# Seven block products in layer 0 as well, with two weight sums made by accumulating transfers

## The chip, the cores and the metric

The kernel runs on one core of a Trainium2 chip. The metric is the time of one execution on the device in microseconds (us), the median of several runs. The engines are TensorE (PE; its weight loads are shown apart as PEld), VectorE (DVE), ScalarE (ACT), GpSimd (POOL) and SyncE (SP), which issues the plain transfers.

## The reference

A decoder trunk of two layers on 512 tokens of width 1024, all in float32. Every sub-layer is modulated by a conditioning vector `c`: six vectors a layer, shift, scale and gate for the mixer and for the FFN. The FFN hidden size is 2816, which the kernel takes as 22 tiles of 128.

```python
cond = jax.nn.silu(c)
for l in range(DEPTH):
    mod = cond @ ada_w[l] + ada_b[l]
    sh1, sc1, g1, sh2, sc2, g2 = [m[:, None, :] for m in jnp.split(mod, 6, axis=-1)]
    h = _rms_norm(x, norm_mix[l]) * (1.0 + sc1) + sh1
    y = _even_mixer(h, ...) if l % 2 == 0 else _odd_mixer(h, ...)
    x = x + g1 * (y @ w_out[l])
    h = _rms_norm(x, norm_ffn[l]) * (1.0 + sc2) + sh2
    x = x + g2 * _swiglu(h, ffn_gate[l], ffn_up[l], ffn_down[l])

def _swiglu(h, wg, wu, wd):
    return (jax.nn.silu(h @ wg) * (h @ wu)) @ wd
```

## The kernel before

**Products.** Activations lie transposed, features on the partitions, tokens along the row. A float32 product is made from three fast ones: each operand is split into a high part in the format `float32r` and the rest, and high x high, high x low and low x high are summed in PSUM (`mm3`). The split of a weight is a copy on ScalarE into `w` (the high part) and a subtraction, mostly on DVE, into another `w`.

**Weights.** They come as units of up to 128x2048 into one of three buffers `raw` (`load_to`, issued on SP), are split ahead of their use into buffers `w` of 128x1024 (`prep_to`; 13 of them), and are taken by `unit`.

**FFN.** Each layer's FFN runs in two parts of eleven tiles (`FPARTS`): gate and up for eleven hidden tiles, then the down projection over them (`reduce_out` with `gv` 5), whose result is added to `x`. A direct tile (`ffn_tile`) is 8 blocks x 2 x 3 products over 512 columns. In layer 1, tiles 3 to 21 (`SEVEN`, `DIRECT`) go another way: the weights [gate, up] and the two halves of the rows and of the tokens are seen as 2x2 blocks, and seven block products (Winograd's form) take the place of eight (`ffn_seven`). Each block product is 4 blocks x 3 products over 256 columns. It needs sums of weight blocks, made in `prep_seven` on DVE from the four quarters q0 to q3 of `raw` (s13 = [q0 + q2, q3 + q2], then q2 = q0 + q2 + q3 in `raw` and q1 = q2 + q1), and sums of activation blocks, made once a layer in `combos` from a float32 copy `hf` of the normed activations.

**Modulation.** The first two vectors of layer 0 come at the start. The others are made in the background, by generators `mod_rest`: vectors 2, 3 and 4 of layer 0 beside its mixer, and vector 5 of layer 0 and all six of layer 1 beside the FFN of layer 0. There a vector is four transfers of 1 MB into `raw` and sixteen DVE instructions over 512 columns (`raw` x `cond` added up), in nine steps; `run_bg(n)` takes n steps. It is called after each FFN tile and each output tile of the down projection.

**Order.** The program first records its operations with their costs, and a list scheduler (`Sched`) then writes each engine's order: operations become ready when what they need has ended by its costs, a buffer from a pool must be free, and the operation with the lowest number comes first (on DVE the one that is due first). A group has a number of buffers and a reserve: its last so many buffers go only to the tile that is next in program order. The engines then follow this order as it stands, and semaphores make them wait.

Of the kernel before, what the change touches and what calls it, by code (L numbers as in the profile page):

```python
# [12 lines left out]
AF = mybir.ActivationFunctionType  # L13
OP = mybir.AluOpType
# [3 lines left out]
P = 128  # L18
# [7 lines left out]
BIG = 1e30  # L26
NW, NT2 = 13, 59

SEVEN, DIRECT = (1,), 3
TOPK = 128  # L30
# [50 lines left out]
class View:  # L81
    __slots__ = ("base", "chain")
# [70 lines left out]
class Op:  # L153
    __slots__ = ("eng", "dur", "fn", "preds", "succs", "prio", "tiles", "left", "ready", "start", "end", "idx", "name")

# [6 lines left out]
class Sched:  # L162
# [13 lines left out]

    def op(self, eng, dur, fn, outs, ins):
        o = Op()
        o.idx = len(self.ops)
        o.eng, o.dur, o.fn, o.prio = eng, dur, fn, o.idx + self.shift  # L180
# [28 lines left out]

    def lat(self, a, b, raw):  # L210
        if a.eng == b.eng:
            if a.eng in ("PE", "SP"):
                return 0
            return self.SAME if raw else 0
        if a.eng == "SP":
            return self.DMA
        return self.CROSS
# [154 lines left out]
class Kern:  # L372
    def __init__(self, ctx, tc, io, out):
        self.ctx, self.tc, self.nc, self.io, self.out = ctx, tc, tc.nc, io, out
        pool = lambda n, b, **k: ctx.enter_context(tc.tile_pool(name=n, bufs=b, **k))
        self.const = pool("const", 1)
        self.s = s = Sched(tc)
        s.group("raw", pool("raw", 3), 3, 0, None)
        s.group("w", pool("w", NW), NW, 0, None)
        n = NT2  # L380
        s.group("t2", pool("t2", n), n, 8, None, L=12, pT=4, qf=3, q=8, nt=10, hid=26, ada0=20, T=18)
        s.group("sm", pool("sm", 80), 80, 16, None)
        s.group("ps", pool("ps", 8, space=PSUM), 8, 1, None, mm=3, lg=2, tp=2, pv=2, gu=6, st=7)
        self.bg = []
# [124 lines left out]
    def dma(self, out, src, cols):  # L509
        self.s.op("SP", 60 + cols * 512 / 360.0, lambda: self.nc.sync.dma_start(out.ap(), src), [out], [])  # L510

# [9 lines left out]
    def stream(self):  # L521
# [11 lines left out]
        self.units = u  # L533
        self.raws, self.ws = {}, {}
        self.loaded = self.prepped = self.cursor = 0

    def load_to(self, n):
        while self.loaded < min(n, len(self.units)):
# [5 lines left out]
            self.dma(t[:, :w], src, w)  # L544
            self.raws[self.loaded] = t
            self.loaded += 1

# [30 lines left out]
    def prep_seven(self, i, raw):  # L578

        q = raw.rearrange("p (q c) -> p q c", q=4)  # L580
        s13 = self.s.tile("w", "w", (P, 1024))
        s13v = s13.rearrange("p (q c) -> p q c", q=2)
        two = lambda: [self.s.tile("w", "w", (P, 1024), FR) for _ in range(2)]
        halves = lambda t: [t[:, a:a + 512] for a in (0, 512)]
        self.tt(s13v, q[:, 0::3], q[:, 2][:, None].to_broadcast([P, 2, 512]), OP.add)
        xh, xl = two()
# [536 lines left out]
    def reduce_out(self, l, B, gv, halves, last):  # L1123
# [11 lines left out]
        def one(m, c):  # L1135
# [7 lines left out]
            self.s.shift = 0  # L1143
            self.run_bg(2)
        n = 4 if halves else 8
# [19 lines left out]

    def combos(self):

        c1, c2 = HALVES
        T = []
        for k in range(8):  # L1170
            t = self.hf[k]
            self.act(t, t, AF.Identity, bias=self.mod[1][:, 3, k:k + 1])
        for k in range(4):
# [50 lines left out]
    def ffn(self, l, H, last):  # L1224
        T = None
        for pi, (a, b) in enumerate(FPARTS):
# [11 lines left out]
            for f, c in jobs:  # L1238
                if l not in SEVEN or f < DIRECT:
                    sg = self.ffn_tile(H, f, c, w(f), hid[f - a])  # L1240
                else:
                    T = T or self.combos()
                    sg = self.ffn_seven(H, T, w(f), hid[f - a])
                self.lnexp = []
                if l == 0 and f == FT - 1:
                    self.act_table([sg])
                self.run_bg(2)
            self.reduce_out(l, hid, 5, pi == 1, last if pi == 1 else lambda m, c: None)
# [125 lines left out]
```

## Time and profile before

| | |
|---|---|
| median of three runs | 1195.34 us (1194.95 to 1197.35) |
| profiled execution | 1196.39 us |
| its span, first to last instruction | 1194.3 us |
| PE busy | 1170.6 us, 98% |
| PE weight loads busy | 979.6 us, 82% |
| DVE busy | 817.6 us, 68% |
| ACT busy | 554.9 us, 46% |
| POOL busy | 84.3 us, 7% |
| read from HBM | 148.41 MB, 126 GB/s over the span |

The profile is one execution; its own time stands beside its span, since the span leaves out what lies before the first and after the last instruction. An engine's share is an average over stages with different limits. In the trace `L433` is the matmul, `L459` ScalarE's activation, `L475` the two-operand operation of DVE or POOL, `L490` the operation with a scalar and two tensors, `L483` that with scalars alone, `L510` the transfer issued by SP. In the changed kernel these lines are 436, 462, 478, 493, 486 and 513, and the accumulating transfer is `L517`.

### The profile page before, as it was taken

To read this page: it belongs to the slowest core of one execution; us is meant where nothing else is said; L and a number is where in the kernel's file an instruction comes from. 1 tells how busy PE (TensorE), PEld (TensorE's weight loads), DVE (VectorE), ACT (ScalarE), POOL (GpSimd) and SP (SyncE) were. 2 spreads that over 40 slices of the span, in tenths; PEclk is the share of its full clock that TensorE was granted. 3 is DMA by queue.
4 is the path that set the end of the run, shared out by engine and by line. 5 is a ranking of instruction groups with operands and counts; after the bars stand their busy time and mean duration, and the time that the engine had idled before them with its cause. 6 is when DMAs were issued, how large, how long until landed. Compare 5 with 4: busy or idle time off the path is not lost.

```text
span 1194.3 us, 18348 instructions
## 1 busy us (share of the span) xinstructions
PE 1170.6 (98%) x7108; PEld 979.6 (82%) x7108; DVE 817.6 (68%) x1832; ACT 554.9 (46%) x1305; POOL 84.3 (7%) x224
## 2 busy tenths in 40 slices
PE   6989899999999999999999999999999999999998
PEld 3867677669988888888889976668999988999988
DVE  5589999847975466555543867765999844788831
ACT  5554276855532322233232647764766532566510
POOL 0132223300000000000000021100000000000000
PEclk9999999999999999999999999999999999999999
DMA  9635614202475456644432131112123332233401
GB/s 349 240 135 177 221 63 142 71 1 71 144 285 206 141 194 243 215 176 147 165 130 71 71 106 36 72 36 71 51 92 106 124 121 91 72 106 107 158 37 36
DMA packets 32423, 151.68 MB, mean 127 GB/s; under 512 B 3152, under 2 KB 4304, under 8 KB 21072
## 3 DMA queue, kind: packets, MB, share of 16 engines
q1 hardware_dynamic: 32336, 150.52, 35.7%
q8 instruction: 55, 0.90, 0.3%
q14 instruction: 32, 0.26, 0.1%
HBM read 148.41 MB, written 2.10 MB: 126 GB/s over the span
## 4 chain that ended last, share of the span: by engine, by line
PE 86%; DVE 5%; ACT 1%; POOL 0%; issue 0%
PE ps L433 82%; PE ps L444 3%; DVE t L910 1%; DVE t L490 1%; DVE sm L909 1%; DVE w L475 1%; ACT t L459 0%; DVE t L475 0%; DVE t L495 0%; POOL sm L475 0%; DVE sm L501 0%; DVE t L483 0%; ACT sm L459 0%; POOL sm L483 0%; DVE sm L490 0%
## 5 line engine op out<-in xcount | busy, mean ns | idle before, releaser
L433 PE MATMUL ps<-t,w 128*128 128x256 f32 (+2 forms) x4980 | 833.7, 328 | 0.9 <-DVE w L475 0.4
L433 PEld LDWEIGHTS ps<-t,w 128*128 128x128 f32 x4980 | 735.4, 190 | 86.0 <-issue 5.3
L475 DVE TENSOR_TENSOR w<-raw,w 128x512 fp32r<-128x512 f32 (+1 forms) x340 | 235.4, 726 | 136.3 <-PE ps L433 105.2
L459 ACT ACTIVATE w<-raw 128x512 fp32r<-128x512 f32 (+1 forms) x364 | 217.1, 645 | 153.8 <-PE ps L433 126.4
L459 ACT ACTIVATE t<-ps 128x256 f32<-128x256 f32 (+6 forms) x331 | 137.9, 447 | 289.7 <-PE ps L433 235.7
L433 PE MATMUL ps<-w,t 128*128 128x512 f32 (+1 forms) x768 | 189.9, 391 | 1.3 <-DVE t L490 1.3
L433 PEld LDWEIGHTS ps<-w,t 128*128 128x128 f32 x768 | 133.6, 190 | 36.7 <-issue 9.3
L490 DVE SCALAR_TENSOR_TENSOR x<-ps,mod,x 128x512 f32<-128x512 f32 (+1 forms) x64 | 39.4, 616 | 74.3 <-PE ps L433 74.1
L490 DVE SCALAR_TENSOR_TENSOR t<-raw,cond,t 128x512 f32<-128x512 f32 x112 | 77.3, 746 | 17.3 <-DMA raw<-in_ada 17.2
L433 PE MATMUL ps<-t,t 64*128 64x256 f32 (+5 forms) x592 | 86.5, 356 | 1.4 <-ACT t L459 0.8
L433 PEld LDWEIGHTS ps<-t,t 64*128 64x128 f32 (+2 forms) x592 | 56.2, 186 | 32.7 <-issue 18.5
L475 DVE TENSOR_TENSOR t<-t,t 128x256 f32<-128x256 f32 (+3 forms) x124 | 66.7, 555 | 20.4 <-ACT t L459 20.2
L475 DVE TENSOR_TENSOR t<-ps,t 128x256 f32<-128x256 f32 (+4 forms) x158 | 66.1, 440 | 19.0 <-ACT t L459 12.7
L444 PE MATMUL ps<-cst,t 128*128 128x128 f32 x388 | 61.2, 278 | 9.4 <-DVE t L475 7.0
L459 ACT ACTIVATE t<-t,sm 128x256 f32<-128x256 f32 (+3 forms) x128 | 65.5, 514 | 9.3 <-DVE sm L495 7.6
L444 PEld LDWEIGHTS ps<-cst,t 128*128 128x128 f32 x388 | 45.0, 140 | 29.4 <-ACT t L459 7.3
L495 DVE CUSTOM_DVE_ANT_0 t<-ps,cst 128x256 f32<-128x256 f32 (+3 forms) x104 | 39.2, 408 | 25.6 <-PE ps L433 25.3
L459 ACT ACTIVATE t<-t 128x256 f32<-128x256 f32 (+3 forms) x82 | 43.8, 540 | 27.8 <-DVE t L475 27.1
L483 POOL TENSOR_SCALAR sm<-sm 128x8 f32<-128x8 f32 (+2 forms) x64 | 16.6, 260 | 488.8 <-DVE sm L501 468.9
L459 ACT ACTIVATE t<-t,mod 128x256 fp32r<-128x256 f32 (+2 forms) x64 | 32.5, 556 | 23.6 <-DVE t L490 23.5
L475 POOL TENSOR_TENSOR w<-raw,w 128x512 fp32r<-128x512 f32 x24 | 33.8, 1418 | 127.7 <-PE ps L433 75.8
L459 ACT ACTIVATE t<-x 128x256 f32<-128x256 f32 (+1 forms) x44 | 22.5, 511 | 39.5 <-DVE x L490 36.7
(74 smaller groups left out, 548.7 us busy)
## 6 DMA issues: line engine op xcount, KB each, us to landing
raw<-in_wg SPq DMA_DIRECT2D x44, 1024.0 KB, 4.8
raw<-in_ada SPq DMA_DIRECT2D x40, 1024.0 KB, 5.2
raw<-in_wd SPq DMA_DIRECT2D x20, 1024.0 KB, 4.8
raw<-in_w0c SPq DMA_DIRECT2D x10, 1024.0 KB, 6.5
t<-in_ada SPq DMA_DIRECT2D x32, 256.0 KB, 6.6
raw<-in_wo SPq DMA_DIRECT2D x8, 1024.0 KB, 4.9
raw<-in_w1c SPq DMA_DIRECT2D x6, 1024.0 KB, 4.7
x<-in_x SPq DMA_DIRECT2D x8, 256.0 KB, 4.2
```

What stands on the lines that cost most here:

```text
L433: self.nc.tensor.matmul(o.ap(), l.ap(), r.ap(), start=st, stop=sp, skip_group_check=True)
L444: self.s.op("PE", 107, lambda: self.nc.tensor.transpose(out.ap(), src.ap(), self.ident.ap()), [out], [src, self.ident])
L459: self.nc.scalar.activation(out.ap(), src.ap(), func, **kw)
L475: lambda: self.eng(e).tensor_tensor(out.ap(), a.ap(), b.ap(), op=op), [out], [a, b])
L483: self.eng(e).tensor_scalar(out.ap(), a.ap(), val(s1), val(s2), op0=op0, **kw)
L490: lambda: self.eng(e).scalar_tensor_tensor(out.ap(), a.ap(), val(s), b.ap(), op0=op0, op1=op1),
L495: lambda: self.nc.vector.tensor_tensor_reduce(out.ap(), a.ap(), b.ap(), op0=OP.add, op1=OP.min, scale=scale, scalar=3e38, accum_out=accum. ...
L909: self.s.op("DVE", 65 + 1.05 * n, lambda m8=m8: self.nc.vector.max(m8.ap(), sc.ap()), [m8], [sc])
L910: self.s.op("DVE", 65 + 1.05 * n, lambda m8=m8: self.nc.vector.match_replace(sc.ap(), m8.ap(), sc.ap(), -3e38), [sc], [m8, sc])
```

## The change

- `SEVEN` becomes (0, 1): tiles 3 to 21 of layer 0 go through `ffn_seven` too, so `norm_tile` keeps `hf` there and `combos` runs for layer 0.
- The sum s13 is made elsewhere, in both layers: behind each such unit `load_to` sends q0 and q3 once more into a tile `d` of 128x1024 (two buffers), on SP, and two accumulating transfers from GpSimd's queue add q2 to each half. `prep_seven` takes `d` for its s13 and its first DVE addition goes.
- The buffers `w` become 11, with a reserve of 3; `d` takes the room of the two.
- The background takes one step after each FFN tile (before: two) and four after each output tile of a down projection (before: two).
- The scheduler counts a transfer's latency by a mark of the operation instead of the engine SP.

```diff
-NW, NT2 = 13, 59
+NW, ND, NT2 = 11, 2, 59
-SEVEN, DIRECT = (1,), 3
+SEVEN, DIRECT = (0, 1), 3
+NBG = (1, 4)
...
     def lat(self, a, b, raw):
+        if a.dma:
+            return self.DMA
         if a.eng == b.eng:
...
-        if a.eng == "SP":
-            return self.DMA
...
-        s.group("w", pool("w", NW), NW, 0, None)
+        s.group("w", pool("w", NW), NW, 3, None)
+        s.group("d", pool("d", ND), ND, 0, None)
...
+    def dma_add(self, out, src, cols):
+        self.s.op("POOL", 1000 + cols * 512 / 360.0,
+                  lambda: self.nc.gpsimd.dma_start(out.ap(), src, accum_op=OP.add), [out], [out], True)
...
             self.raws[self.loaded] = t
+            if self.seven(self.loaded):
+
+                d = self.s.tile("d", "d", (P, 1024))
+                self.dma(d[:, :512], src[:, :512], 512)
+                self.dma(d[:, 512:], src[:, 1536:], 512)
+                for a in (0, 512):
+                    self.dma_add(d[:, a:a + 512], src[:, 1024:1536], 512)
+                self.sums[self.loaded] = d
...
-        s13 = self.s.tile("w", "w", (P, 1024))
-        s13v = s13.rearrange("p (q c) -> p q c", q=2)
+        s13 = self.sums.pop(i)
...
-        self.tt(s13v, q[:, 0::3], q[:, 2][:, None].to_broadcast([P, 2, 512]), OP.add)
...
-            self.run_bg(2)
+            self.run_bg(NBG[1] if gv == 5 else 2)
...
-    def combos(self):
+    def combos(self, l):
...
-            self.act(t, t, AF.Identity, bias=self.mod[1][:, 3, k:k + 1])
+            self.act(t, t, AF.Identity, bias=self.mod[l][:, 3, k:k + 1])
...
-                self.run_bg(2)
+                self.run_bg(NBG[0])
```

On DVE, in the second part of layer 0's gate and up tiles, there stood before the splits of direct weights (`w<-raw,w`), the steps of the modulation (`raw,cond`) and the ends of tiles:

```order
L475 TENSOR_TENSOR w<-raw,w 128x512 x2
L490 SCALAR_TENSOR_TENSOR t_5275<-raw,cond,t_5275 128x512
L490 SCALAR_TENSOR_TENSOR t_5271<-raw,cond,t_5271 128x512
L490 SCALAR_TENSOR_TENSOR t_5275<-raw,cond,t_5275 128x512
L475 TENSOR_TENSOR t_5319<-ps,t_5319 128x512
L475 TENSOR_TENSOR mod_96<-ps,smt 128x8
L475 TENSOR_TENSOR t_5380<-t_5319,t_5373 128x512
```

At about the same place stands now, in the changed kernel (`d` holds s13; `raw<-d,raw` and `raw<-raw` are the two sums that stay on DVE; `ps` and `t` are the sums of products):

```order
L478 TENSOR_TENSOR raw<-raw 128x512
L478 TENSOR_TENSOR w<-raw,w 128x512
L493 SCALAR_TENSOR_TENSOR t_6127<-raw,cond,t_6127 128x512
L478 TENSOR_TENSOR w<-raw,w 128x1024
L478 TENSOR_TENSOR w<-raw,w 128x512
L478 TENSOR_TENSOR raw<-d,raw 128x512
L478 TENSOR_TENSOR w<-d,w 128x1024
L478 TENSOR_TENSOR ps<-ps,t_6242 128x256
L478 TENSOR_TENSOR raw<-raw 128x512
L478 TENSOR_TENSOR t_6031<-ps,t_6005 128x256
```

A modulation step that stood among others now stands alone between the sums and splits of a tile, and a sum in PSUM stands behind the two readers of `d`.

On SP, in the same part, gate/up weights and modulation weights alternated before:

```order
L510 DMA raw<-in_wg 128x2048
L510 DMA raw<-in_ada 128x2x1024
L510 DMA raw<-in_wg 128x2048
L510 DMA raw<-in_ada 128x2x1024
L510 DMA raw<-in_wg 128x2048
```

In the changed kernel two quarters of a unit follow, each into half of a `d`:

```order
L513 DMA raw<-in_wg 128x2048
L513 DMA d<-in_wg 128x512 x2
L513 DMA raw<-in_ada 128x2x1024
L513 DMA raw<-in_wg 128x2048
L513 DMA d<-in_wg 128x512 x2
L513 DMA raw<-in_wg 128x2048
L513 DMA d<-in_wg 128x512
L513 DMA raw<-in_ada 128x2x1024
L513 DMA d<-in_wg 128x512
```

Once a modulation load stands between the two halves of a `d`, and there are fewer such loads among the tiles.

On POOL, between the last splits of layer 0's mixer and the first statistics of layer 1's, stand now the accumulating transfers:

```order
L478 TENSOR_TENSOR w<-raw,w 128x512 x4
L517 DMA d<-in_wg 128x512 x38
L486 TENSOR_SCALAR sm<-sm 128x4
```

Before, nothing stood there. The 38 are those of 17 tiles of layer 0 (the first two tiles' four stand earlier, within the mixer) and of the first two of layer 1; 34 more stand behind layer 1's mixer.

## Rows read from the trace of the kernel before

**Rows 1.** Page, parts 1 and 4: busy time by engine; the chain's shares.

```profile
PE 1170.6 (98%) x7108; PEld 979.6 (82%) x7108; DVE 817.6 (68%) x1832; ACT 554.9 (46%) x1305; POOL 84.3 (7%) x224
...
PE 86%; DVE 5%; ACT 1%; POOL 0%; issue 0%
```

**Rows 2.** Windows by stage: busy us (instructions) of each engine, granted clock, DMA share, GB/s.

```profile
core 0: us, PE busy (x) PEld busy (x) DVE busy (x) ACT busy (x) POOL busy (x), PEclk, DMA share, GB/s
0.00:269.40 269.40, 251.66 (x1531) 180.55 (x1532) 216.12 (x614) 151.97 (x426) 61.46 (x146) 0.98 0.43 155
269.40:322.90 53.50, 53.50 (x403) 51.50 (x402) 42.74 (x93) 27.56 (x57) 2.55 (x2) 1.00 0.28 97
...
333.70:422.40 88.70, 88.70 (x404) 72.22 (x403) 51.25 (x83) 28.71 (x54) 0.00 (x0) 1.00 0.55 191
422.40:484.20 61.80, 61.80 (x286) 49.92 (x285) 40.43 (x66) 14.68 (x26) 0.00 (x0) 1.00 0.64 227
484.20:607.40 123.20, 123.20 (x560) 100.19 (x559) 63.40 (x104) 35.29 (x66) 0.00 (x0) 1.00 0.51 179
...
811.30:866.80 55.50, 55.34 (x413) 53.04 (x414) 43.88 (x97) 34.68 (x70) 0.00 (x0) 1.00 0.22 73
866.80:877.70 10.90, 10.90 (x51) 9.00 (x50) 10.62 (x20) 5.30 (x10) 0.00 (x0) 1.00 0.13 35
...
1018.20:1129.20 111.00, 111.00 (x925) 110.85 (x924) 95.39 (x152) 66.95 (x124) 0.00 (x0) 1.00 0.30 105
```

**Rows 3.** Windows: three direct tiles of layer 0; eleven seven-product tiles of layer 1.

```profile
518.07:550.71 32.64, 32.64 (x145) 27.03 (x144) 15.38 (x25) 10.86 (x20) 0.00 (x0) 1.00 0.36 129
1018.19:1129.25 111.06, 111.06 (x925) 110.91 (x924) 95.45 (x152) 66.95 (x124) 0.00 (x0) 1.00 0.30 105
```

**Rows 4.** Timeline of ScalarE from 517.5 to 529.5 us: start, length, instruction, idle before.

```profile
518.07 0.60 ACT L459 ACTIVATE t<-ps 128x512 f32<-128x512 f32 x1 [4.94 <-PE ps L433]
...
528.95 0.60 ACT L459 ACTIVATE t<-ps 128x512 f32<-128x512 f32 x1 [4.69 <-PE ps L433]
529.45 0.62 ACT L459 ACTIVATE w<-raw 128x512 fp32r<-128x512 f32 x1
```

**Rows 5.** DVE's instruction groups, 1018.2 to 1129.2 us: xcount, busy us, mean ns.

```profile
L475 DVE TENSOR_TENSOR w<-raw,w 128x512 fp32r<-128x512 f32 x39 | 25.9, 685 | 0.2 <-PE ps L433 0.2
...
L475 DVE TENSOR_TENSOR w<-raw 128x1024 f32<-128x1024 f32 x10 | 12.2, 1219 | 5.5 <-PE ps L433 5.3
```

**Rows 6.** DVE's instruction groups, 484.2 to 607.4 us (second part, layer 0).

```profile
L490 DVE SCALAR_TENSOR_TENSOR t<-raw,cond,t 128x512 f32<-128x512 f32 x32 | 22.1, 746 | 4.1 <-DMA raw<-in_ada 4.1
...
L483 DVE TENSOR_SCALAR t<-raw,cond 128x512 f32<-128x512 f32 x4 | 1.8, 486 | 1.0 <-DMA raw<-in_ada 1.0
```

**Rows 7.** DVE's instruction groups, 422.4 to 484.2 us (down projection of the first part).

```profile
L490 DVE SCALAR_TENSOR_TENSOR t<-raw,cond,t 128x512 f32<-128x512 f32 x24 | 16.5, 746 | 1.7 <-DMA raw<-in_ada 1.7
...
L483 DVE TENSOR_SCALAR t<-raw,cond 128x512 f32<-128x512 f32 x4 | 1.8, 480 | 0.0
```

**Rows 8.** Page, part 6, DMA issues: KB each, median us from issue to landing.

```profile
raw<-in_wg SPq DMA_DIRECT2D x44, 1024.0 KB, 4.8
...
t<-in_ada SPq DMA_DIRECT2D x32, 256.0 KB, 6.6
...
x<-in_x SPq DMA_DIRECT2D x8, 256.0 KB, 4.2
```

**Rows 9.** Windows, the first 40 us: columns as in rows 2.

```profile
0.00:40.00 40.00, 29.70 (x199) 17.17 (x200) 22.84 (x66) 19.33 (x35) 0.20 (x4) 1.00 0.97 361
```

**Rows 10.** Waits of DVE, 333.7 to 607.4 us: total us, times, longest.

```profile
DVE t L490 <- DMA raw<-in_ada: 17.2, 7, 3.3
```

**Rows 11.** Waits of PE, 0 to 269.4 us: total us, times, longest.

```profile
PE ps L433 <- DVE w L475: 0.4, 1, 0.4
```

More of the change, by code (lines that the diff above doesn't have):

```diff
@@ L153 @@
 class Op:
-    __slots__ = ("eng", "dur", "fn", "preds", "succs", "prio", "tiles", "left", "ready", "start", "end", "idx", "name")
+    __slots__ = ("eng", "dur", "fn", "preds", "succs", "prio", "tiles", "left", "ready", "start", "end", "idx", "dma")
 class Group:
@@ L175, in tile, with op @@
         return VTile(group, tag, shape, dt)
-    def op(self, eng, dur, fn, outs, ins):
+    def op(self, eng, dur, fn, outs, ins, dma=False):
         o = Op()
+        o.dma = dma
         o.idx = len(self.ops)
@@ L509, in dma @@
     def dma(self, out, src, cols):
-        self.s.op("SP", 60 + cols * 512 / 360.0, lambda: self.nc.sync.dma_start(out.ap(), src), [out], [])
+        self.s.op("SP", 60 + cols * 512 / 360.0, lambda: self.nc.sync.dma_start(out.ap(), src), [out], [], True)
+    def dma_add(self, out, src, cols):
+        self.s.op("POOL", 1000 + cols * 512 / 360.0,
+                  lambda: self.nc.gpsimd.dma_start(out.ap(), src, accum_op=OP.add), [out], [out], True)
     def store(self, dst, src, cols):
@@ L533, in stream @@
         self.units = u
-        self.raws, self.ws = {}, {}
+        self.raws, self.ws, self.sums = {}, {}, {}
         self.loaded = self.prepped = self.cursor = 0
@@ L1241, in ffn @@
                 else:
-                    T = T or self.combos()
+                    T = T or self.combos(l)
                     sg = self.ffn_seven(H, T, w(f), hid[f - a])
```

## The prediction

> **What bounds the kernel now.** I read the page's busy shares and its chain first [rows 1]: TensorE is busy for 98% of the span and carries 86% of the chain that ended last. A busy PE can hide waits, because an instruction that waits counts as busy, so I next cut the span into stages [rows 2]. In the two gate/up stretches of layer 0 (333.7 to 422.4 and 484.2 to 607.4 us) PE is busy from end to end, the granted clock is 1.00, VectorE (DVE) works 51.25 of 88.70 us and 63.40 of 123.20 us, and DMA is at about half (0.55 and 0.51). So these stretches last as long as their matmuls do. In the seven-product stretch of layer 1 (1018.2 to 1129.2) PE is again busy throughout, its weight loads too (110.85 of 111.00), but DVE works 95.39 of 111.00 us, which is 86%. That is the stretch to learn from: layer 0 gets the same products, and in it 86% of DVE cost PE nothing.
>
> **The products.** A direct tile is 48 matmuls of 512 columns, a seven-product tile 84 of 256 columns. The SiLU that ends one direct tile of layer 0 starts at 518.07 and the next at 528.95 [rows 4]: 10.88 us for a tile. The window over three of them, with 144 weight loads, is 32.64 us [rows 3] and gives the same. The seven-product window holds 924 matmuls, 11 tiles, in 111.06 us: 10.10 us a tile. The change turns 19 tiles of layer 0 (3 to 21), so it takes off 19 x (10.88 - 10.10) = **15 us**. Nothing else takes matmuls away.
>
> **The sums by transfer.** In layer 1 one DVE addition of 128x1024 for each tile disappears: 1219 ns each, 12.2 us for the ten in the window [rows 5]. PE did not wait for DVE there, so this earns nothing in layer 1; it is what makes room in layer 0. In its place each of the 38 seven-product tiles gets four transfers of 256 KB: two plain ones on SP's queue and two accumulating ones on GpSimd's, which otherwise has nothing to do in these stretches (POOL 0.00 in [rows 2]). What is queued behind them is only more of them; what waits for them is the DVE addition of `d` into `raw` and the copy of `d` on ScalarE. In the order of the changed kernel the first of these stands, in layer 1's steady tiles, 59 matmuls behind the second accumulating transfer, and 47 at the tightest place in layer 0: at 111.06 us / 924 = 0.12 us a matmul that is 7.1 and 5.6 us. The trace has no accumulating transfer. Its nearest rows are 256 KB plain transfers, which land 4.2 us after issue, or 6.6 us where DMA is saturated [rows 8]; a 1 MB one takes 4.8. From below I take 4.2 (no wait at all), from above two that follow each other, 6.6 + 4.2 = 10.8 us. I choose the lower end, because DMA is nowhere saturated in layer 1 and the two go out together: **0**. The Trainium skill (DMA: Bandwidth & Descriptors, Anatomy of one DMA) gives a transfer from GpSimd 2.0 us plus its bytes over 436 GB/s, an estimate of 2.6 us here; by it the term would be 0 too, and no run here shows it yet.
>
> **DMA in layer 0.** Counting both queues' orders, the seven tiles from the first of the second part on ask for 23 MiB in 637 matmuls, some 71 us at the prices above: 338 GB/s. The highest sustained rate in the trace is 361 GB/s at a share of 0.97, in the first 40 us [rows 9], so this is 91% of what can be had (372). SP issues in order, DVE takes the modulation steps in order, and already before DVE waited 17.2 us for modulation weights in this part of the program [rows 10]. If an accumulating byte costs one transfer, the loss is near nothing. If it costs two, the 4.25 MiB of GpSimd count double, 27.25 MiB need 77 us at 372 GB/s, and the stretch loses 5.5 us. I take **1.5 us**. The Trainium skill (Collectives: The Full Stack, The bandwidth ceiling) says why an add may cost double: it needs two source reads, and a reduction ran at half the rate of a copy. By it the term is the upper one, 5.5 us; no row of this trace bears on it.
>
> **DVE in layer 0.** A seven-product tile without its large addition costs DVE (95.39 - 12.2) / 11 = 7.56 us. A modulation step keeps DVE 0.69 us (22.1 us for 32), and 0.45 us where it begins a sum (1.8 us for 4) [rows 6, 7]. In DVE's order of the changed kernel I count 24 of them (four begin a sum) in the first part's eight seven-product tiles and 32 (four) in the second part's eleven. So the gate/up parts need 8 x 7.56 + 15.6 = 76 of 81 us, and 83.2 + 21.1 = 104 of 111 us: **94%** in both, where it was 58 and 51%. In the down projection between them 28 steps [rows 7] become 43, which makes 40.43 + 10 = 50 of 61.80 us, 81%, and leaves room. DVE has been kept 97% busy (10.62 of 10.90 us in [rows 2]), so 94% is not yet the bound by itself, but it leaves 5 and 7 us for waits of any kind. From 0 to 7 us; I take **1 us**, near the lower end, since at 86% nothing was lost.
>
> **The first tiles.** The combinations of the activations (ACT 16 instructions, DVE 24) come into layer 0 beside tiles 0 to 2. The same work in layer 1 lies in 811.3 to 866.8, where PE is busy 55.34 of 55.50 us and DVE 43.88: hidden, **0** (up to 2 if the cover is thinner in layer 0, where DVE had 42.74 of 53.50 and loses modulation steps in exchange).
>
> **Two weight buffers fewer.** 13 become 11, of which the planner keeps the last three for the tile that is next in program order. In the seven-product tiles this is even, since the large sum no longer sits in one of them. In the attention stages, eight changes of weights of 512 columns each find two halves prepared where there was room for more. PE waited 0.4 us for `w` in the first 269 us [rows 11]; at worst each change shows one split, 0.62 us on ScalarE [rows 4] and 0.69 on DVE [rows 5], 10 us in all. The nearest row is the 0.4, so I take **1.5 us**.
>
> **Sum.** -15.0 + 0 + 1.5 + 1 + 0 + 1.5 = -11. The profiled execution took 1196.39 us (span 1194.3 and 2.1 around it) and becomes 1185.4; the median of the runs lies 1.05 us below it, so I predict **1184.3 us**. A difference of 0.2%, 2.4 us, is about what a measurement of this kernel can tell from none.
>
> **Rivals.**
> 1. *Transfers or DVE fill up in layer 0.* The 5.5 us of DMA and the 7 us of DVE come instead of 1.5 and 1: PE shows gaps before evacuations and splits. For it: 94% and 91%. Against it: PE at the new price is slower than DVE, and what is late first, modulation weights, is not needed until layer 1. Time: with the double price of the accumulating bytes alone 1184.3 + 4 = 1188 us, with DVE's loss on top 1194; chance 0.22, of which 0.13 still clearly faster and 0.09 within 0.2%. The Trainium skill (Collectives: The Full Stack, The bandwidth ceiling) leads one to expect the double price.
> 2. *Slower: the accumulating transfers land late.* The DVE addition that reads `d` blocks everything behind it, the next being a sum in PSUM that PE needs. Each microsecond beyond 7.1 after issue is then paid at about 34 tiles (38 less those loaded long ahead). At 0.44 us beyond, 7.5 us, the 15 us are gone; at 8.0 the kernel takes 1184 + 31 = 1215 us. For it: 6.6 us is in the trace, and the second transfer follows the first. Against it: 4.2 and 4.8 where DMA is not full. Chance 0.15.
> 3. *All of it is hidden.* None of the small losses appears and the two weight buffers cost nothing: 1195.3 - 15 - up to 2 = 1178 to 1180. The part below 1179 has chance 0.08.
>
> **Chances.** The forecast, 1179 to 1190: 0.55. With rival 3 and the faster part of rival 1 that makes 0.76 faster, 0.09 the same, 0.15 slower. The range reaches from 1178 (rival 3) to 1197 (rival 1 and the beginning of rival 2); about 0.05 lies below it and 0.15 above.
>
> **What would show it.** Right: 84 matmuls of 256 columns in about 10.1 us in layer 0 from tile 3 on, PE busy from end to end, DVE at 90 to 96% of these stretches, DVE's waits for `d` near zero, accumulating transfers that land within 7 us, and a start of the layer 0 FFN within 2 us of before. Wrong: waits of DVE or ACT for `d` of more than 0.4 us a tile (rival 2); gaps of PE released by DVE or a DMA share near 0.95 in the second part (rival 1); an attention stage that is several us longer (the buffers).

## The result, and the profile after

The changed kernel takes **1226.61 us** (median of four runs, 1222.86 to 1233.49) where the kernel before, run beside it on the same chip, takes 1195.25. The ratio is 1.0268, with an interval from 1.0245 to 1.0292: slower, outside the range that was forecast. The profiled execution is the longest of the four, 1233.49 us, 37.1 us more than the profiled execution of before.

The page of the changed kernel: parts 1, 3, 4, 5 and 6 (in part 6 the size of one transfer and the median us from issue to landing).

```profile
PE 1177.2 (96%) x7792; PEld 1015.9 (82%) x7792; DVE 885.1 (72%) x1970; ACT 612.0 (50%) x1416; POOL 151.9 (12%) x300
...
q1 hardware_dynamic: 43280, 170.45, 39.1%
q0 software_dynamic: 10944, 19.93, 9.9%
...
PE 67%; DVE 14%; DMA 13%; issue 3%; ACT 1%; POOL 1%; SPq 0%; DVEq 0%; POOLq 0%; ACTq 0%
...
L517 POOL DMA_DIRECT2D d<-in_wg x76 | 67.3, 1030 | 585.9 <-DVE t L478 205.2
...
L478 DVE TENSOR_TENSOR raw<-d,raw 128x512 f32<-128x512 f32 x38 | 26.2, 689 | 53.2 <-DMA d<-in_wg 46.7
...
raw<-in_wg SPq DMA_DIRECT2D x44, 1024.0 KB, 5.8
...
d<-in_wg SPq DMA_DIRECT2D x76, 256.0 KB, 5.1
d<-in_wg POOLq DMA_DIRECT2D x76, 256.0 KB, 6.7
```

TensorE's share of the chain was 86% [rows 1] and is 67%. DMA, which had no share there, has 13%. Before the 38 additions that read `d`, DVE stood idle for 53.2 us, 46.7 of them ended by the landing of a transfer into `d`.

The windows by stage of the changed kernel, which answer to [rows 2]: the three direct tiles, the first part's seven-product tiles in layer 0, its down projection, the second part, and layer 1's second part; columns as there.

```profile
268.00:321.20 53.20, 53.20 (x417) 52.00 (x416) 41.78 (x89) 32.21 (x64) 3.80 (x3) 1.00 0.28 90
332.10:426.60 94.50, 86.04 (x687) 83.55 (x687) 76.64 (x133) 49.13 (x96) 12.32 (x14) 0.98 0.79 234
426.60:488.80 62.20, 62.20 (x291) 50.42 (x290) 47.95 (x76) 15.24 (x25) 1.76 (x2) 1.00 0.76 262
488.80:619.00 130.20, 118.76 (x948) 114.70 (x947) 106.48 (x183) 64.81 (x125) 17.63 (x20) 0.97 0.84 251
1041.60:1166.30 124.70, 116.93 (x925) 116.29 (x924) 83.52 (x140) 65.39 (x124) 14.14 (x16) 0.95 0.59 161
1064.00:1076.00 12.00, 9.36 (x67) 9.16 (x67) 5.74 (x12) 5.21 (x10) 1.75 (x2) 0.86 0.75 193
```

The stretch that was to gain nothing lost most: the same 924 matmuls of layer 1 took 111.0 us [rows 2] and take 124.70, although DVE works 83.52 us there and no longer 95.39. In layer 0 the two gate/up stretches were to fall from 88.7 and 123.2 us to some 81 and 111; they rise to 94.5 and 130.2. Of the 37.1 us between the two profiled executions, 14.0 lie in layer 0's feed-forward, 5.2 in layer 1's mixer with its output projection, 3.7 and 15.8 in the two parts of layer 1's feed-forward with their down projections; what comes before is 1.6 us shorter.

One of the three stalls of layer 1's second part, in the chain of work that ended last, in order of time (start, length, what):

```profile
1052.94 6.13 PE ps L436 x51
...
1059.85 0.54 POOL d L517
1060.39 8.41 DMA d<-in_wg
1068.80 0.02 issue
1068.83 0.04 DVE raw L478
1068.86 0.57 issue
1069.44 0.44 DVE ps L478
1069.87 0.02 issue
1069.89 0.39 ACT t L462
1070.29 0.04 issue
1070.33 9.77 PE ps L436 x68
```

Read it from the bottom: PE goes on at 1070.33, when ScalarE has read a PSUM sum; ScalarE waited for DVE's addition in PSUM (1069.44), and that stood in DVE's queue behind `raw<-d,raw` (1068.83), which waited for the second accumulating transfer. That one landed 8.41 us after its issue. The same chain's next link back is the first accumulating issue at 1059.85. The waits of DVE and of PE in the whole stretch (1041.6 to 1166.3: total us, times, longest):

```profile
DVE raw L478 <- DMA d<-in_wg: 13.2, 3, 4.9
```

```profile
PE ps L436 <- ACT t L462: 7.8, 3, 3.1
```

The three gaps of PE, from the start of one matmul to the start of the next, are 2.92, 3.34 and 2.35 us, 8.6 in all, or 8.25 more than three steps of 0.12. After each of them PE ran 12 to 25 matmuls at 213 ns instead of 120, at the lower of its two clock levels (1.2 instead of 2.4 GHz; the granted clock is 0.50 from 1070.0 to 1073.4 us, and 0.86 on the mean of 1064 to 1076). The trace has 55 such matmuls in the stretch, 55 x 0.093 = 5.1 us. Gaps and clock together are 13.3 of the 13.7 us that this stretch lost.

And the round of one `d` buffer, in SP's queue from 1053 to 1080 (the loads into `d` are issued in pairs, one for each half):

```profile
1054.00 0.81 SPq L513 DMA_DIRECT2D d<-in_wg  x2
1060.75 0.33 SPq L513 DMA_DIRECT2D raw<-in_wg  x1
1064.08 0.87 SPq L513 DMA_DIRECT2D d<-in_wg  x2
1074.95 0.33 SPq L513 DMA_DIRECT2D raw<-in_wg  x1
1078.31 0.80 SPq L513 DMA_DIRECT2D d<-in_wg  x2
```

The buffer loaded at 1054.00 takes its next load at 1078.31. In between lie the plain loads (5.8 us), the accumulating pair (9.0, from 1059.85 to 1068.80) and the hold until DVE's last reading ends (9.5). In the steady tiles of layer 1's first part the three are 5.0 to 5.3, 8.5 and 8.5, some 22 us. With two buffers that is a new tile every 11 to 12 us; the mean in the second part is 124.7 / 11 = 11.3, where PE needs 10.1.

### The profile page after: what moved, and what is told of

It is laid out like the page before. It is cut to its first block, busy times and chain, and to the rows that moved or that the text cites. A ratio compares the mean times of both kernels' runs of the same rounds, so it can differ in the third digit from the quotient of the medians.

```text
span 1231.7 us, 20420 instructions
## 1 busy us (share of the span) xinstructions
PE 1177.2 (96%) x7792; PEld 1015.9 (82%) x7792; DVE 885.1 (72%) x1970; ACT 612.0 (50%) x1416; POOL 151.9 (12%) x300
## 3 DMA queue, kind: packets, MB, share of 16 engines
q1 hardware_dynamic: 43280, 170.45, 39.1%
q0 software_dynamic: 10944, 19.93, 9.9%
## 4 chain that ended last, share of the span: by engine, by line
PE 67%; DVE 14%; DMA 13%; issue 3%; ACT 1%; POOL 1%; SPq 0%; DVEq 0%; POOLq 0%; ACTq 0%
PE ps L436 63%; DMA d<-in_wg 8%; DVE t L493 4%; PE ps L447 3%; DVE w L478 3%; DMA raw<-in_ada 3%; DVE t L923 2%; DVE t L478 2%; DVE sm L922 2%; DVE t L498 1%; ACT t L462 1%; DMA raw<-in_wg 1%; POOL d L517 1%; DMA raw<-in_w0s 1%; DVE t L486 0%
## 5 line engine op out<-in xcount | busy, mean ns | idle before, releaser
L436 PEld LDWEIGHTS ps<-t,w 128*128 128x128 f32 x5664 | 772.4, 195 | 84.7 <-ACT t L462 22.2
L462 ACT ACTIVATE w<-raw 128x512 fp32r<-128x512 f32 (+1 forms) x364 | 227.5, 669 | 156.4 <-PE ps L436 119.7
L478 DVE TENSOR_TENSOR w<-raw,w 128x512 fp32r<-128x512 f32 (+1 forms) x340 | 249.2, 759 | 64.2 <-PE ps L436 33.0
L462 ACT ACTIVATE t<-ps 128x256 f32<-128x256 f32 (+6 forms) x388 | 153.7, 426 | 249.9 <-PE ps L436 155.7
L517 POOL DMA_DIRECT2D d<-in_wg x76 | 67.3, 1030 | 585.9 <-DVE t L478 205.2
L478 DVE TENSOR_TENSOR t<-t,t 128x256 f32<-128x256 f32 (+3 forms) x163 | 84.4, 541 | 25.8 <-ACT t L462 25.5
L462 ACT ACTIVATE t<-t 128x512 fp32r<-128x512 f32 (+3 forms) x109 | 56.0, 523 | 26.9 <-DVE t L478 26.1
L478 DVE TENSOR_TENSOR raw<-d,raw 128x512 f32<-128x512 f32 x38 | 26.2, 689 | 53.2 <-DMA d<-in_wg 46.7
L462 ACT ACTIVATE w<-d 128x1024 fp32r<-128x1024 f32 x38 | 40.1, 1056 | 27.2 <-PE ps L436 16.2
L478 DVE TENSOR_TENSOR w<-d,w 128x1024 fp32r<-128x1024 f32 x38 | 46.3, 1220 | 4.6 <-PE ps L436 3.3
```

Of the source, the lines that this page charges most:

```text
L436: self.nc.tensor.matmul(o.ap(), l.ap(), r.ap(), start=st, stop=sp, skip_group_check=True)
L462: self.nc.scalar.activation(out.ap(), src.ap(), func, **kw)
L478: lambda: self.eng(e).tensor_tensor(out.ap(), a.ap(), b.ap(), op=op), [out], [a, b])
L517: lambda: self.nc.gpsimd.dma_start(out.ap(), src, accum_op=OP.add), [out], [out], True)
```

## The experiments

Times are medians; ratios are against the kernel before, run beside it on the same chip. The planner is the list scheduler that writes the engines' orders. "Layer 0's feed-forward" is the profiled time from the last update of x in its output projection to the last one in its second down projection: 370.3 us before, 384.3 in the changed kernel.

### Layer 1 and the accumulating transfers

**Seven products in layer 0 undone.** `SEVEN = (1,)`, and the old rate of modulation.

```diff
-SEVEN, DIRECT = (0, 1), 3
-NBG = (1, 4)
+SEVEN, DIRECT = (1,), 3
+NBG = (2, 2)
```

> Sums by accumulating transfers, two d and eleven w, but seven products in layer 1 alone and the modulation steps where they were. Loop and DMA theory: layer 1 is as slow as in the changed kernel, 1212 to 1220. If layer 1 was slow for something that layer 0 left behind: 1195 to 1199.

1217.74 us, ratio 1.0185 (1.0159 to 1.0212). Layer 0's feed-forward is back at 370.2 us; in layer 1's second part a matmul still takes 136 ns on the mean, where it took 120 before. So some 22 us are lost with layer 0 as it was, by the sums by transfer and the two `w` fewer; the next runs tell these apart.

**The transfers without their addition.** GpSimd's transfers copy; the sums are not formed, so the products are not the reference's.

```diff
-lambda: self.nc.gpsimd.dma_start(out.ap(), src, accum_op=OP.add)
+lambda: self.nc.gpsimd.dma_start(out.ap(), src)
```

> The changed kernel, but the two transfers from GpSimd copy instead of adding (the quarter q2 takes the place of each sum, so the additions are left out). Loop theory with a dear accumulation: the pair lands in 5 to 6 us in place of 8.5, the loop is about 19 us for two tiles, under 20.2, layer 1's second part is 111 to 113 us and the kernel takes 1190 to 1203. If it is GpSimd's issue that is slow and not the addition: the pair lands as late as before and the time stays at 1223 to 1230.

1194.63 us, 0.9991 (0.9971 to 1.001). The same bytes, issues and order, and 32 us less. From its page (queue, part 6) and its windows of layer 0's and layer 1's second part:

```profile
q0 software_dynamic: 6080, 19.93, 5.9%
...
d<-in_wg POOLq DMA_DIRECT2D x76, 256.0 KB, 4.3
```

```profile
481.50:602.20 120.70, 115.88 (x956) 112.65 (x955) 107.52 (x184) 66.10 (x125) 10.75 (x20) 1.00 0.79 271
1017.00:1127.90 110.90, 110.90 (x926) 110.90 (x925) 83.48 (x139) 66.06 (x124) 8.60 (x16) 1.00 0.55 181
```

A transfer lands in 4.3 us, not 6.7, and layer 1's second part has no loss (110.90 us), with the same 11 `w`. But layer 0's feed-forward is 367.3 us: of the 15 us it keeps 3. That is a second cause, which the additions don't explain.

**A third `d` buffer**, for one `w` buffer.

```diff
-NW, ND, NT2 = 11, 2, 59
+NW, ND, NT2 = 10, 3, 59
```

> Three buffers d in place of two, ten w in place of eleven. Loop theory (a buffer d is busy for 5.3 us of loading, 8.5 of accumulating and about 9 of being held, 22.8 us for two tiles, 11.4 a tile): three buffers give 7.6 a tile, less than PE's 10.1, so the second part of layer 1 returns from 124.7 to about 111 us, its first from 86.9 to about 82, layer 0 loses most of its waits too, and the kernel takes 1187 to 1197. DMA theory (the accumulating bytes fill the transfer engines): the same as the changed kernel, 1223 to 1230. DVE theory (DVE is full in layer 0): layer 1 returns, layer 0 does not, about 1207.

1211.86 us, 1.013 (1.0097 to 1.0163): half of the loss comes back, and none of the three cases fits. Layer 1's second part takes 119.9 us. The planner counts 2.3 us to the landing of any transfer. With a third buffer it places the addition that reads `d` earlier, when PE has done 0.88 of a tile's matmuls, where before it was 0.26 or 0.57 of the next tile's. DVE still waits for the landing there, 12.5 us in six places.

**The third buffer, and a true figure in the planner's table**: 4.7 us behind an accumulating transfer, 2.3 behind any other.

```diff
         if a.dma:
-            return self.DMA
+            return self.DMA + 2400 * (a.eng == "POOL")
```

> Three d buffers, 10 w, and the planner told that what follows an accumulating transfer comes 4.7 us behind it instead of 2.3, so that the additions that read d stand later in DVE's order. If the loop of d buffers and the early read were the whole loss of layer 1: a step there at 120 to 123 ns, 1194 to 1199 in all. If the accumulating transfers cost by their load on the DMA engines: 1208 to 1214, as with three buffers alone (1211.9).

1197.90 us, 1.0018 (1.0005 to 1.0031). The transfers land no sooner (6.5 us by the page), but the trace has no wait of DVE for them in layer 1's second part, which takes 110.90 us again:

```profile
1022.00:1132.90 110.90, 110.90 (x926) 110.87 (x925) 84.90 (x140) 68.12 (x124) 12.36 (x14) 1.00 0.59 167
```

Layer 0's feed-forward is still 380.1 us, 12.8 more than with plain transfers, and its second part loses as before:

```profile
484.90:612.90 128.00, 118.92 (x959) 115.79 (x958) 108.69 (x184) 65.53 (x125) 17.68 (x20) 0.97 0.90 269
```

The DMA share there is 0.90. The true figure with two `d` buffers was not run, so what the third buffer does by itself beside it is not shown.

### What limits layer 0

**All sums on DVE again**, no `d`, 13 `w`, seven products in both layers, the new rate of modulation.

```diff
-NW, ND, NT2 = 11, 2, 59
+NW, ND, NT2 = 13, 2, 59
...
+        s13 = self.s.tile("w", "w", (P, 1024))
+        s13v = s13.rearrange("p (q c) -> p q c", q=2)
...
+        self.tt(s13v, q[:, 0::3], q[:, 2][:, None].to_broadcast([P, 2, 512]), OP.add)
```

> The sums back on DVE in both layers, 13 buffers w, no d and no accumulating transfer; seven products in both layers and the moved modulation steps stay. Loop and DMA theory: layer 1 as before the change (111 us for its second part); in layer 0 DVE needs 8.66 us a tile and the steps, 85 of 81 us and 116 of 111, so at 97% busy 88 and 120 us against 88.7 and 123.2: 1188 to 1194. DVE theory: in-order waits make it worse than direct tiles, 1198 or more.

1195.93 us, 1.0009 (0.9999 to 1.0019), between the two cases. Layer 1 is within 1.1 us of before in each stage; layer 0's feed-forward is 368.4 us.

**Modulation steps 16 columns wide** (on the kernel with plain transfers; the modulation vectors are not the reference's).

```diff
-self.stt(acc[g], src, self.cond[:, k:k + 1], acc[g], ...)
+self.stt(acc[g][:, 0:16], src[:, 0:16], self.cond[:, k:k + 1], acc[g][:, 0:16], ...)
```

> The kernel with plain transfers (the additions left out), and in it the modulation steps that run on DVE beside layer 0's feed-forward reduced from 512 to 16 columns, so that those modulation vectors are wrong; their transfers, their order and their hold on the three raw buffers stay. Theory A (DVE, over 87% busy there, is what keeps layer 0 from its 15 us): layer 0's feed-forward falls from 367 us to 352 to 356, the whole to 1180 to 1184. Theory B (transfers and the three raw buffers are it): layer 0 stays at 364 to 368, the whole at 1192 to 1195.

1186.98 us, 0.9935 (0.992 to 0.995); layer 0's feed-forward 361.4 us, between the two theories. A modulation step falls from 750 to 229 ns, and 6 of the missing 12 us come back: DVE's time counts, but is not all.

**Modulation without its transfers** (the same kernel, the steps read a constant).

```diff
-                        src = t[:, 1024 * e + 512 * g:1024 * e + 512 * (g + 1)]
+                        src = self.smt
```

> The kernel with plain transfers again, and in it the modulation steps on DVE kept at full width, but reading a constant tile: the modulation vectors' 28 MB of transfers beside layer 0's feed-forward and their raw buffers are left out, and the vectors are wrong. Theory A (DVE busy): layer 0's feed-forward stays at 364 to 368 us, the whole at 1192 to 1195. Theory B (transfers and raw buffers): 352 to 356 us, the whole 1180 to 1184. If neither run falls by 8 us, the two limits stand at about the same height.

1197.70 us, 1.0029 (1.0013 to 1.0045). The run does not tell the two apart. With nothing to wait for, the planner put 112 of the 128 steps ahead of layer 0's feed-forward, where they made the first stage 14 us longer (298.6 to 312.6 us); the feed-forward, with 16 steps left, took 357.8. What it does show: the second part, with no modulation beside it, takes 120.4 ns from one seven-product matmul to the next, as in layer 1. The first part takes 120.6, though the 16 steps stand among its tiles (347.8 to 414.9 us): at full width, with nothing to wait for and with DVE at 67.04 of 75.20 us (89%), they cost PE next to nothing.

**A fourth raw buffer**, paid for with four `t2` tiles, and with one `w` and two `t2` (again on plain transfers).

```diff
-s.group("raw", pool("raw", 3), 3, 0, None)
+s.group("raw", pool("raw", 4), 4, 0, None)
```

> The kernel with plain transfers (the additions left out) with a fourth raw buffer, paid for by four of 59 t2 tiles. If the three raw buffers are the link between the modulation's DVE time and the weights' loads: layer 0's feed-forward 367 us falls to 357 to 361, 1185 to 1189 in all. If DVE alone decides: it stays at 365 to 368. Four t2 tiles fewer may cost elsewhere (mixers), which the stages show.

> The same fourth raw buffer, paid for by one w buffer and two t2 tiles. The same two cases: 357 to 361 or 365 to 368 us for layer 0's feed-forward; if it agrees with the run that pays with t2 tiles, what was given up is not the cause.

1221.25 us (1.0213) and 1201.50 us (1.0052); layer 0's feed-forward 392.4 and 373.0. Both are slower than with three raw buffers, and the two disagree by 19 us in layer 0's feed-forward, so what was given up cannot be left out of account. Nothing follows for the raw buffers.

**The two sums computed on GpSimd.**

```diff
...
-self.tt(s13v, q[:, 0::3], ..., OP.add)
+self.tt(s13v, q[:, 0::3], ..., OP.add, e="POOL")
```

> Seven products in both layers with the two sums computed by a GpSimd addition of 2x512 columns instead of by transfers (no d buffers, 13 w buffers, 3 in reserve). By the 1418 ns of GpSimd's 512-column subtraction one takes some 2.8 us, 95 us in all, on an engine that is idle in the feed-forward. Theory A (DVE is layer 0's limit): like the kernel with DVE sums in layer 1 and 8 to 12 us better in layer 0, 1183 to 1188. Theory B: the raw buffer is held 1.7 us longer and nothing is gained, 1195 to 1200. If GpSimd and DVE slow each other, over 1200 and longer DVE rows.

1215.18 us, 1.0165 (1.015 to 1.018). The third case of the expectation came. POOL's timeline in layer 1, and DVE's at the same time:

```profile
1079.14 2.49 POOL L477 TENSOR_TENSOR w<-raw 128x1024 f32<-128x1024 f32 x1 [8.49 <-PE ps L435]
```

```profile
1079.71 2.48 DVE L477 TENSOR_TENSOR w<-raw,w 128x512 fp32r<-128x512 f32 x1 [0.33 <-ACT w L461]
```

A subtraction that takes DVE 0.68 us took 2.48 beside GpSimd's addition; 9 of the 41 in this stretch took that long or longer, each under such an addition, and none of the others did.

### The place of the modulation

**Four of layer 1's vectors moved out**: 2 to 4 into layer 1's mixer, 5 into its feed-forward, with three `d` buffers and the true figure, and with all sums on DVE.

```diff
-self.bg = [self.mod_rest(0, 5, False)] + [self.mod_rest(1, v, False) for v in range(6)]
+self.bg = [self.mod_rest(0, 5, False)] + [self.mod_rest(1, v, False) for v in (0, 1)]
...
```

> The kernel with three d buffers and the honest 4.7 us in the planner, and layer 1's modulation vectors 2, 3 and 4 moved from layer 0's feed-forward into layer 1's mixer, vector 5 into layer 1's feed-forward: three of seven vectors stay beside layer 0's seven products. If the modulation beside layer 0's feed-forward (its DVE time and its hold on the raw buffers together) is what takes the 15 us there: layer 0's feed-forward falls from 380 us to 360 to 366, the mixer of layer 1 gains 0 to 6 us (DVE is 70% busy there, DMA 17%), 1180 to 1188 in all. If the accumulating transfers alone hold layer 0: no change, 1196 to 1200.

> The same move in the kernel with all sums on DVE (13 w buffers, no d). Layer 0's feed-forward from 368 us to 356 to 360, layer 1's mixer up by 0 to 6, layer 1's feed-forward up by 0 to 3 (86% of DVE and one vector more): 1184 to 1192 in all. If DVE is too full with sums and vector 5 in layer 1's first part, 1192 to 1197.

1197.19 us (1.0009, 0.9998 to 1.0021) and 1208.19 us (1.0102); both miss in all, though layer 0's feed-forward did what was expected. With the transfers, layer 0's feed-forward falls from 380.1 to 360.4 us, and its second part, which now has no modulation beside it, takes 110.8 us for 924 matmuls, the 10.1 us a tile that were forecast:

```profile
483.20:594.00 110.80, 110.80 (x925) 110.80 (x924) 84.97 (x140) 68.11 (x124) 17.70 (x20) 1.00 0.74 202
```

But layer 1's mixer with its output projection pays 10.6 us (170.7 to 181.3) and its first part with the down projection 6.6. With all sums on DVE, layer 0's feed-forward falls from 368.4 to 358.6 us, and layer 1 pays 14.0 and 7.6 in the same two places.

**No vector moved away, but none issued between the tiles**: of the second part (first and third run), of both parts (second and fourth: vector 5 goes ahead into layer 0's output projection).

```diff
-                self.run_bg(NBG[0])
+                self.run_bg(NBG[0] if pi == 0 else 0)
```

```diff
+            if l == 0:
+                self.bg = [self.mod_rest(0, 5, False)]
             self.reduce_out(l, Y, 2, True, after(1, l))
+            self.drain_bg()
...
-                self.run_bg(NBG[0])
```

> The kernel with three d buffers and the honest 4.7 us in the planner (1197.9), and in layer 0's second part no step of the modulation is issued between the seven-product tiles: vector (0,5) and the next one stay in the first part, three and a half in the first down projection, the rest in the second (no vector moves into layer 1). If modulation between the tiles is the cause: second part with its down projection from 189.4 us to 171 to 175, 1180 to 1186 in all. If the total of DVE and transfer work over the feed-forward is the cause, wherever it is issued: 1193 to 1198.

> The same and vector (0,5) moved ahead into layer 0's output projection, so that neither part of layer 0's feed-forward has modulation between its tiles (five of ten w buffers in reserve instead of three, which the planner needs to find an order). First part with its down projection from 190.7 us to 178 to 184, the output projection of layer 0 up by 0 to 8: 1172 to 1184 if the modulation between the tiles is the cause; like the run without this move if the output projection pays for what the first part gains.

> All sums on DVE, seven products in both layers (1195.9), and no modulation between the tiles of layer 0's second part. If the place of the modulation is the cause: 1184 to 1189. If DVE's whole load in layer 0 is the cause: 1193 to 1197.

> All sums on DVE, and no modulation between the tiles of either part of layer 0's feed-forward: vector (0,5) in layer 0's output projection, layer 1's six in the two down projections. If the place is the cause: 1174 to 1184. If DVE's whole load is: 1192 to 1197.

Three `d` buffers: 1196.87 us (1.0003, 0.9993 to 1.0013) and 1188.27 (0.9936, 0.9924 to 0.9948). Sums on DVE: 1189.70 us (0.995, 0.9938 to 0.9962) and **1184.27 (0.9904, 0.9891 to 0.9917)**. The last is the fastest kernel of the study, 11 us ahead of the kernel before. By the figures of its expectation the first run falls into the second case, the load wherever it is issued; the others come out 0.3 to 4.3 us above the first case, the place. But the edits did not clear the tiles: the planner orders by due times, and 20 to 24 steps stayed among the second part's tiles in all four.

**Half the rate in the first down projection**, and **the last placement with direct tiles in layer 0**, as in the kernel before (the expectation calls them twelve products).

```diff
-            self.run_bg(NBG[1] if gv == 5 else 2)
+            self.run_bg(4 if gv == 5 and halves else 2)
```

```diff
-SEVEN, DIRECT = (0, 1), 3
+SEVEN, DIRECT = (1,), 3
```

> The version with all sums on DVE and no modulation between the tiles (1184.3), with the modulation issued at half the rate in layer 0's first down projection and the rest in the second: 16 modulation steps still ran beside the second part's tiles there, at a mean step of 125 ns. If the modulation steps among the tiles are what is left: the second part at 120 to 121 ns a step, 1178 to 1182 in all. If not: 1184 again.

> The same placement of the modulation, rate of four in the first down projection, with twelve products in layer 0 as in the kernel before. If the gain of 11 us came from the placement alone: 1184 to 1187. If it came from the seven products, which the placement only lets through: 1192 to 1196, since twelve products left DVE room.

1193.10 us (0.9975, 0.9964 to 0.9987) and 1196.55 us (1.0007, 0.9998 to 1.0016). The placement alone gives nothing; the gain is that of the seven products. The run at half the rate meets neither case. Its second part takes 120.0 ns from one seven-product matmul to the next, as expected, and layer 0's feed-forward is at its shortest, 351.0 us; but 29 steps ran over into layer 1's mixer, which took 187.1 us instead of 173.3.

The series with sums on DVE, counted in the traces (modulation steps that DVE starts between the first and the last 256-column matmul of the two parts):

| placement | steps beside the tiles | layer 0's feed-forward, us | whole, us |
|---|---|---|---|
| as in the change | 62 | 368.4 | 1195.93 |
| none issued in the second part | 43 | 363.7 | 1189.70 |
| none issued in either part | 21 | 357.8 | 1184.27 |
| half the rate in the first down projection | 5 | 351.0 | 1193.10 |

From first to last that is (368.4 - 351.0) / 57 = 0.31 us of feed-forward for each step taken away, of the 0.75 that a step takes. DVE in the second part and its modulation groups there, sums on DVE, placement as in the change (67 of the 991 matmuls are other work, 512 columns of the down projection in the main):

```profile
478.50:606.60 128.10, 123.77 (x991) 119.03 (x990) 121.14 (x200) 66.45 (x128) 0.00 (x0) 1.00 0.51 180
...
L492 DVE SCALAR_TENSOR_TENSOR t<-raw,cond,t 128x512 f32<-128x512 f32 x33 | 22.9, 744 | 0.0
L485 DVE TENSOR_SCALAR t<-raw,cond 128x512 f32<-128x512 f32 x6 | 2.6, 477 | 0.0
```

The same with half the rate:

```profile
476.20:588.40 112.20, 112.20 (x931) 111.94 (x930) 97.86 (x156) 66.89 (x125) 0.00 (x0) 1.00 0.37 127
...
L492 DVE SCALAR_TENSOR_TENSOR t<-raw,cond,t 128x512 f32<-128x512 f32 x6 | 4.4, 745 | 0.0
```

All waits of DVE in the first of these two stretches:

```profile
DVE w L477 <- PE ps L435: 3.0, 4, 1.6
DVE t L477 <- PE ps L435: 2.8, 6, 1.1
DVE ps L477 <- PE ps L435: 0.8, 1, 0.8
```

It waits for PE alone, 6.6 us, and never for a modulation load. So in this kernel it is DVE's own time, 121.14 of 128.10 us (95%), that holds PE back; at 97.86 of 112.20 (87%) PE is busy from end to end.

## Why the prediction was wrong

**The step that failed: "The sums by transfer", "I choose the lower end ... 0".** It bounded the landing by 4.2 and 10.8 us and took 4.2, with 7.1 us of slack. Measured from each transfer's own issue, the first of a pair lands after a median of 4.5 us, the second after 7.85; from the first issue to the second landing it is 8.5 in layer 1's steady tiles. Of the reasons given, "DMA is nowhere saturated in layer 1" held for the mean of the stretch (a share of 0.59) and not where it mattered: while the pair of 1059.85 was under way beside a 1 MB load (1060.7 to 1067.5 us) the share was 0.85. Of the eight pairs of layer 1's second part, those behind which the next 1 MB load was issued 2.7 us later or more landed in 5.6 to 6.4 us, and those with such a load within 1.1 us in 8.6 to 9.0 (in the first part's steady tiles, with the load 2.4 to 2.7 us behind, in 8.3 to 8.6). The load beside it was not tried apart; the addition was, and without it the page's median is 4.3 us instead of 6.7. The term was not 0 but some 22 us in layer 1 alone (the run with direct tiles in layer 0), and some 32 in the whole kernel (the run with plain transfers).

**Rival 2 is what happened.** It had the mechanism to the letter, the addition that blocks a PSUM sum behind it, and a chance of 0.15. By its price the measured 7.85 us would give 1184.3 + 34 x 0.75 = 1210. It counted the wait on one tile and missed two things: the loop of two `d` buffers, in which load, pair and hold of one buffer must fit in two tiles (some 22 us against 20.2), so that lateness can add up to a gap every few tiles; and the lower clock behind such a gap, 5.1 of 13.7 us. The plain transfers, and the third buffer with a true figure in the planner, each remove the whole loss of layer 1's second part: the late landing is the cause there, and a third buffer with a later place in DVE's order a cure. How much of it the buffer does and how much the place is not shown.

**"The products", -15 us**: right in size. Where modulation was out of the way, layer 0's second part took 110.8 us for eleven tiles, 10.1 each. The best kernel kept 11 of the 15 us.

**"DVE in layer 0", +1 us of 0 to 7, and "DMA in layer 0", +1.5 of 0 to 5.5**: the second failure. Even with the additions left out (plain transfers) layer 0 kept 3 us where these terms left 12.5, a loss of 9.5 us more. With the additions its feed-forward took 17.0 us more than that (384.3 against 367.3), and 12.8 more even with three buffers and the true figure: in layer 0 the cure of layer 1 did not hold. The count of DVE's work was about right (104 of 111 us forecast, 106.48 of 130.20 measured, with 39 steps beside the second part's tiles where 32 were counted), and so was the worry that 94% leaves little for waits; the choice "near the lower end, since at 86% nothing was lost" was the error. Modulation steps stand in DVE's queue among the splits that PE needs. With the sums on DVE each cost PE 0.31 us on the mean, and in the second part that was DVE's own time. With plain transfers DVE was less full, 107.52 of 120.70 us (89%), and it and ScalarE also waited for transfers in layer 0's second part (482.5 to 602.1):

```profile
DVE raw L478 <- DMA d<-in_wg: 4.7, 3, 2.2
ACT w L462 <- DMA raw<-in_wg: 3.5, 3, 1.9
ACT w L462 <- DMA d<-in_wg: 3.0, 2, 1.9
DVE raw L478 <- DMA raw<-in_wg: 2.1, 2, 1.8
```

How much of the loss is DVE's time there, and how much the late weights, of which modulation loads share SP's queue and the three raw buffers, stays open: narrow steps gave back 6 us, the run without modulation loads moved the steps, the runs with a fourth buffer disagree.

The doubled price of an accumulating byte, from which the upper end of the DMA term was worked out, is in the trace as time of the DMA engines: 19.93 MB took 9.9% of 16 engines' span, 0.50% a MB, where the hardware queue's took 39.1 / 170.45 = 0.23% and GpSimd's plain copies of the same bytes 5.9 / 19.93 = 0.30%. The Trainium skill (Collectives: The Full Stack, The bandwidth ceiling) led to expect half the rate, and the trace agrees roughly: 2.2 times the one, 1.7 times the other. The estimate of 2.6 us for such a transfer that the Trainium skill gives (DMA: Bandwidth & Descriptors, Anatomy of one DMA) does not hold beside this kernel's other transfers: medians of 4.3 us plain, 6.7 accumulating.

**"The first tiles", 0, and "Two weight buffers fewer", +1.5**: small as forecast. In the direct tiles' stretch PE is busy throughout (53.20 of 53.20 us), and it ended 1.7 us earlier than before. Layer 1's mixer with its output projection took 5.2 us more in the changed kernel (178.8 instead of 173.6), but 170.7 with ten `w` and three `d`, so the `w` buffers are not what it lacked; what did it was not tried apart. The modulation in the first down projection stayed hidden: DVE has 47.95 of 62.20 us (77%, where 81% was forecast), and the stretch was 61.80 us before.

## What to carry to other kernels

Before work goes to a transfer that changes data in place, lay out the whole round of its buffer, load, change, hold, and compare it with the buffers' number times the tile; and give a planner that orders by latency the latency of that transfer, not of a plain one. An engine that takes its work in order and is busy for 95% of a stretch can be its bound when work that nobody waits for stands among work that somebody does: put the former where the engine has slack (here the projections), and count what runs over into the next stage. Bound a cost that no row shows by its upper end when one late landing blocks a queue: here the loss was open at 38 tiles, and the gain was 0.8 us at each of 19.

## What the runs showed of the hardware

An accumulating 256 KB transfer takes more packets than a plain one: 10944 for 19.93 MB against 6080, and 1.7 times the engines' time. Each accumulating issue keeps GpSimd 1.03 us on the mean, where a plain one keeps it 0.54; the two of a pair overlap, so the 76 took 67.3 us and 41.2.

A GpSimd addition of 128x1024 holds up a DVE subtraction that reads two operands from SBUF: it took 2.48 us instead of 0.68, and ended some 0.55 us after the addition did. The Trainium skill (SBUF — State Buffer, SBUF: two separate sides) states that the two share a port pair that one instruction holds to its end; the trace agrees.

The granted clock fell behind gaps of PE of 2.4 to 3.3 us in layer 1's second part of the changed kernel, for 12 to 25 matmuls that began 0.4 to 1.4 us after PE had gone on, and behind one of 2.0 us in its first part. The gaps of up to 1.5 us in layer 0 of the kernel with plain transfers were not followed by such matmuls, and neither was one of 3.0 us in layer 0 of the changed kernel (at 365.5): in these traces the length of one gap does not tell whether the clock falls.
